# Three HGRN heads in emission order on three engines, and a decayed query moved to GpSimd

## The chip, the core and the metric

One core of a Trainium2 chip runs the whole program. The metric is the device time of one execution in microseconds, as the median of several runs. TensorE (PE) multiplies, VectorE (DVE), ScalarE (ACT) and GpSimd (POOL) do the elementwise work, and SyncE (SP) issues most of the DMAs.

## The reference

The network has two layers over 512 tokens of width 1024. The first layer runs sliding-window attention and four HGRN2 heads side by side, the second runs chunked attention, and each is followed by a gated convolutional FFN. The change touches the HGRN2 heads alone. For one head, with keys and values of width 128:

```python
f = lbh + (1.0 - lbh) * sigmoid(f_logit)          # forget gate
k = 1.0 - f
cum = cumsum(log(f), axis=block)                  # blocks of 32 tokens
q_dec, k_dec = q * exp(cum), k * exp(-cum)
k_end = k * exp(last - cum)
o_intra = causal(q_dec @ k_dec.T) @ v             # inside a block
state = blk_decay[..., None] * state + k_end.T @ v
o = o_intra + q_dec @ state                       # then RMSNorm and gate
```

## The kernel before

Activations lie with features on the partitions and the 512 tokens along the free side. A weight is split into a high and a low part, and a product is three matmuls (`mm3`, L248 to L250). One unit of weights is 128x1024 and serves a projection of 128 features (`feat`): eight steps of three matmuls. When a unit begins, the unit two behind it is prepared (`prep`): a DMA on SP, a cast on ScalarE (L216), a subtraction on VectorE (L217). The tile buffers let the scheduler do that earlier.

The projections are generators in a list. `fill(n)` runs n steps of them, and `need(name)` runs them until one is finished, which also runs the first step of the next one. So the matmuls of the projections are dealt out between the small matmuls of a head.

**One head, `hgrn(h)`.** `hgrn_in(h)` projects the forget gate and the query. `forget` works on the gate: tanh on ScalarE (L700), the gate (L701), the key 1-f on GpSimd (L702), a scan (L703 to L705) that makes the running product F of each block, a small table of block decays (L708 to L711), then for each of four groups of 128 tokens a reciprocal of F (L714) and a product with the key (L715), giving the decayed key `kd`. GpSimd then makes `f2` (L717) and `k2` (L684). `query` makes the decayed query `qd` (L722), a scaled copy `q2` of half of it (L684 on VectorE), and `kt` (L684 on GpSimd).

`hgrn(h)` itself, in the order of the code: eight steps of the list, which finish the next head's forget gate and begin its query; the scores inside a block (L743) and between blocks (L747, L749); the mask (L750, VectorE) and three copies (L756 and L757 on ScalarE, L758 on VectorE) into the tile `sz`, all of which write the same tile in this order; three steps; the transposes of `kt` (L763) and their copy into `keT` (L765, ScalarE); two steps; the state matmuls (L769), which read `keT`; the three states (L775, L777, VectorE); two steps, which finish the next head's query; the output matmuls (L781 from `sz`, L783 from the states); the squares (L788, ScalarE), the inverse root (L789 and L296 to L300, VectorE) and the scaling of the output (L792, ScalarE).

What sets the order is the framework's scheduler. It orders each engine's instructions by their place in the code and by when its own model thinks them ready, so a later instruction may go ahead of an earlier one that waits. The states and the copy into `keT` are marked for earlier issue. Inside a region `manual_schedule(engines=...)` the named engines issue in exactly the order in which the code emits; the other engines, and where outside instructions fall, stay the scheduler's. The kernel uses such a region for its opening already. An engine works through its list in order, and one that waits holds up what is listed behind it.

Of the kernel before, what the change touches and what calls it, by code (L numbers as in the profile page):

```python
# [23 lines left out]
AF = mybir.ActivationFunctionType  # L24
ALU = mybir.AluOpType
PSUM = bass.MemoryType.PSUM

P = 128
T = 512
NT = T // P  # L30
# [6 lines left out]
EPS = 1e-6  # L37
# [3 lines left out]
HB = 32  # L41
# [3 lines left out]
TOK = [slice(t * P, (t + 1) * P) for t in range(NT)]  # L45
# [103 lines left out]
class Net:  # L149
# [490 lines left out]
    def even(self, xs, ib):  # L640

        nc, tc = self.nc, self.tc
        with tc.tile_pool(name="ev", bufs=2) as ep:
# [34 lines left out]
            ob = [obt[h // 2][:, FH[h % 2]] for h in range(4)]  # L678
            mix = [None] * 8
            blk = lambda t: t.rearrange("p (b n) -> p b n", n=HB)  # L680
            quad = lambda t: t.rearrange("p (t b n) -> p t b n", b=P // HB, n=HB)

            def scaled(out, src, by, engine=nc.gpsimd):
                engine.tensor_mul(out, src, by.unsqueeze(3).to_broadcast(list(src.shape)))  # L684


            tabs = [ep.tile([P, NT, 16], F32, tag=f"tab{i}", bufs=1, name=f"tab{i}") for i in range(2)]
# [3 lines left out]
            def hgrn_in(h):  # L691

                ht = lambda i: self.hp.tile([P, D], F32, tag=f"h{i}", name=f"hg{h}{i}")
                h0, h1 = ht(2 * (h % 2)), ht(2 * (h % 2) + 1)
                f2, kk, F, kd = h0[:, FH[0]], h0[:, FH[1]], h1[:, FH[0]], h1[:, FH[1]]
                qd = tl("qd", "qd", 2)
                k2, q2 = (kk[:, z].rearrange("p (t b n) -> p t b n", b=2, n=HB) for z in (A, B))

                def forget(ps):
                    nc.scalar.activation(f2, ps, AF.Tanh, scale=0.5)  # L700
                    nc.vector.tensor_scalar(f2, f2, c1[:, h:h + 1], c0[:, h:h + 1], op0=ALU.mult, op1=ALU.add)  # L701
                    nc.gpsimd.tensor_scalar(kk, f2, -1.0, 1.0, op0=ALU.mult, op1=ALU.add)  # L702
                    nc.vector.tensor_copy(dd[:, ::HB], f2[:, ::HB])  # L703
                    nc.vector.memset(f2[:, ::HB], 0.0)
                    nc.vector.tensor_tensor_scan(F, f2, dd, 0.0, op0=ALU.mult, op1=ALU.add)  # L705

                    tab = tabs[h % 2]
                    nc.vector.tensor_copy(tab[:, :, 1::4], quad(F)[:, :, :, HB - 1])  # L708
                    nc.vector.tensor_mul(tab[:, :, 2:13:10], tab[:, :, 1:14:12], tab[:, :, 5:10:4])
                    nc.vector.tensor_mul(tab[:, :, 3:12:8], tab[:, :, 2:13:10], tab[:, :, 9:4:-4])  # L710
                    nc.vector.tensor_mul(tab[:, :, 15], tab[:, :, 3], tab[:, :, 13])  # L711

                    for t in range(NT):
                        nc.vector.reciprocal(kd[:, TOK[t]], F[:, TOK[t]])  # L714
                        nc.vector.tensor_mul(kd[:, TOK[t]], kd[:, TOK[t]], kk[:, TOK[t]])  # L715

                    nc.gpsimd.tensor_mul(blk(f2), blk(kd), blk(F)[:, :, HB - 1:].to_broadcast([P, T // HB, HB]))  # L717

                    scaled(k2, quad(f2)[:, :, 0:2], tab[:, :, 5:7])

                def query(ps):
                    nc.vector.tensor_mul(qd, ps, F)  # L722

                    scaled(q2, quad(qd)[:, :, 2:4], tabs[h % 2][:, :, 8:10], nc.vector)

                    scaled(quad(F), quad(f2), tabs[h % 2][:, :, 11:15])

                yield from self.feat(xs, forget)
                yield from self.feat(xs, query)
                heads[h] = (f2, kk, q2, F, kd, qd)  # L730

            heads = [None] * 4

            def hgrn(h):


                self.need(f"hg{h}")
                self.fill(8)
                ke, keT, q2, kt, kd, qd = heads[h]
                tab = tabs[h % 2]  # L740
                intra = self.bank("t", 2)
                for t in range(NT):
                    nc.tensor.matmul(intra[:, TOK[t]], kd[:, TOK[t]], qd[:, TOK[t]], start=True, stop=True)  # L743
                far = self.bank("s", 2)
                for t in range(NT):
                    o = t * P
                    nc.tensor.matmul(far[:, o:o + 64], ke[:, TOK[t]], quad(qd)[:, t, 1::2], start=True, stop=True)  # L747

                    nc.tensor.matmul(far[:, o + 64:o + P], keT[:, 64 * t:64 * t + P], q2[:, t], start=True, stop=True)  # L749
                nc.vector.copy_predicated(sz.rearrange("p (t n) -> p t n", n=P),  # L750
                                          cst[:, CC_HM:CC_HM + P].bitcast(I32).unsqueeze(1).to_broadcast([P, NT, P]),
                                          intra.rearrange("p (t n) -> p t n", n=P))

                scaled(quad(kd), quad(qd), tab[:, :, 0:4])
                s4, f4 = quad(sz), quad(far)
                nc.scalar.copy(s4[0:32, :, 1], f4[0:32, :, 0])  # L756
                nc.scalar.copy(s4[64:96, :, 3], f4[64:96, :, 1])  # L757
                nc.vector.tensor_copy(s4[0:64, :, 2:4], f4[0:64, :, 2:4])  # L758
                self.fill(3)

                ps = self.bank("t", 2)
                for t in range(NT - 1):
                    nc.tensor.transpose(ps[:, TOK[t]], kt[:, TOK[t]], self.ident)  # L763
                with self.tc.high_priority(AHEAD):
                    nc.scalar.copy(keT[:, 0:(NT - 1) * P], ps[:, 0:(NT - 1) * P])  # L765
                self.fill(2)
                po, pu = self.bank("po", 1), self.bank("s", 2)
                for t in range(NT - 1):
                    nc.tensor.matmul(pu[:, TOK[t]], keT[:, TOK[t]], ib[t][:, TOK[h]], start=True, stop=True)  # L769
                S = []  # L770
                with self.tc.high_priority(AHEAD):
                    for t in range(NT - 1):
                        S.append(ep.tile([P, P], F32, tag="S", bufs=3, name="S"))
                        if t == 0:
                            nc.vector.tensor_copy(S[0], pu[:, TOK[0]])  # L775
                        else:
                            nc.vector.scalar_tensor_tensor(S[t], S[t - 1], tab[:, t, 15:16], pu[:, TOK[t]],  # L777
                                                           op0=ALU.mult, op1=ALU.add)
                self.fill(2)
                for t in range(NT):  # L780
                    nc.tensor.matmul(po[:, TOK[t]], sz[:, TOK[t]], ib[t][:, TOK[h]], start=True, stop=t == 0)  # L781
                    if t:
                        nc.tensor.matmul(po[:, TOK[t]], kd[:, TOK[t]], S[t - 1], start=False, stop=True)  # L783

                ss, nv = self.small(4, "hs"), self.small(4, "hv")
                for t in range(NT):
                    j = self.sp.tile([P, D], BF16, tag="junk", bufs=1, name="junk")[:, 0:P]
                    nc.scalar.activation(j, po[:, TOK[t]], AF.Square, accum_out=ss[:, t:t + 1])  # L788
                nc.vector.tensor_scalar(nv, ss, -0.5 / P, -0.5 * EPS, op0=ALU.mult, op1=ALU.add)  # L789
                rs = self.rsqrt4(nv)  # L790
                for t in range(NT):
                    nc.scalar.activation(ob[h][:, TOK[t]], po[:, TOK[t]], AF.Copy, scale=rs[:, t:t + 1])  # L792


            rot = {}
# [82 lines left out]
            def gate(h):  # L878
                def turn(ps):
                    sl = tl("g", "sl", 1)  # L880
                    nc.scalar.activation(sl, ps, AF.Tanh, scale=0.5)
                    nc.vector.scalar_tensor_tensor(sl, sl, 1.0, ps, op0=ALU.add, op1=ALU.mult)
                    pt = self.bank("t", 2)
                    for t in range(NT):
                        nc.tensor.transpose(pt[:, TOK[t]], ob[h][:, TOK[t]], self.ident)
                    nc.vector.tensor_mul(sl, sl, pt)
                    mix[4 + h] = mx_tile(4 + h)
                    self.split(sl, *mix[4 + h], hgn[:, h:h + 1])
                return self.feat(xs, turn)
# [7 lines left out]
                self.later(f"qa{c}", rope(f"qa{c}", 0.125))  # L897
            for h in range(4):
                self.later(f"gate{h}", gate(h))
            for h in range(4):  # L900
                hgrn(h)

            def attention():
                work = [(c, g, i) for c in range(4) for g in range(2) for i in range(NT)]
# [245 lines left out]
```

## Time and profile before

| what | value |
|---|---|
| median of 3 runs | 1211.64 us (1211.58 to 1211.75) |
| the profiled execution: its time, its span | 1212.55 us, 1210.8 us |
| busy share of PE, DVE, ACT, POOL | 99%, 54%, 44%, 9% |
| mean granted TensorE clock | 0.998 |
| the HGRN stage, first to last score matmuls and outputs | about 52 to 116 us of the span |

The span is the time between the first and the last instruction of the profiled execution. A matmul's end is modelled, so the distance between starts tells its cost better than its length: 512 columns start about 0.23 us apart. Idle time counts for the end only where TensorE is idle, or where the end of the program waits.

### The profile page before, as it was taken

What the parts mean: (1) busy time and instruction counts of PE and PEld (TensorE: products, weight loads), DVE (VectorE), ACT (ScalarE), POOL (GpSimd) and SP (SyncE); (2) the same over time, 40 slices, a digit from 0 to 9 for tenths busy, and PEclk for the clock granted to TensorE, in tenths of its full rate; (3) what the DMA queues carried; (4) which work ended last, traced back from release to release, by engine and by line L of the source; (5) the groups of instructions that cost most, each with busy time, mean ns of one, the idle gap of its engine ahead of it and who ended that gap; (6) DMA issues with size and microseconds to landing.
All of it is one profiled execution on the core that took longest, in us unless ns stands there. A gap on an engine that the chain in (4) does not pass through costs nothing.

```text
span 1210.8 us, 15381 instructions
## 1 busy us (share of the span) xinstructions
PE 1195.8 (99%) x5789; PEld 979.3 (81%) x5789; DVE 656.1 (54%) x1356; ACT 534.5 (44%) x975; POOL 111.8 (9%) x120
## 2 busy tenths in 40 slices
PE   9999999999999999999999999999999999999997
PEld 5888777888888888888887777778888888888886
DVE  6887795654442244443547857747544422544434
ACT  5434675653332233333556656656533322333331
POOL 1231010500000000001420000004100000000011
PEclk9999999999999999999999999999999999999999
DMA  6414312233222332322233313222333223232211
GB/s 252 140 53 148 97 62 87 73 132 110 89 95 96 104 102 90 105 85 94 91 115 96 94 47 125 88 72 75 122 106 103 88 90 111 95 104 89 95 61 70
DMA packets 35611, 119.54 MB, mean 99 GB/s; under 512 B 4168, under 2 KB 4304, under 8 KB 35536
## 3 DMA queue, kind: packets, MB, share of 16 engines
q1 hardware_dynamic: 34944, 117.49, 29.5%
q8 instruction: 46, 0.75, 0.2%
q10 hardware_dynamic: 592, 1.05, 0.2%
q14 instruction: 29, 0.24, 0.1%
HBM read 115.12 MB, written 2.10 MB: 97 GB/s over the span
## 4 chain that ended last, share of the span: by engine, by line
PE 89%; DVE 3%; issue 3%; ACT 2%; POOL 2%; DMA 1%; SPq 0%; DVEq 0%; ACTq 0%; POOLq 0%
PE ps_mm L248 18%; PE ps_mm L250 18%; PE ps_mm L249 18%; PE ps_s L248 4%; PE ps_s L250 4%; PE ps_s L249 4%; PE ps_po L248 3%; PE ps_po L250 3%; PE ps_po L249 3%; PE ps_po L1030 2%; POOL hw L346 2%; PE ps_t L1019 1%; PE ps_mm L1084 1%; PE ps_s L1001 1%; PE ps_s L1002 1%
## 5 line engine op out<-in xcount | busy, mean ns | idle before, releaser
L217 DVE TENSOR_TENSOR wl<-wr,wh 128x1024 fp32r<-128x1024 f32 (+1 forms) x187 | 232.5, 1246 | 313.3 <-ACT wh L216 308.6
L216 ACT CAST wh<-wr 128x1024 fp32r<-128x1024 f32 x194 | 200.0, 1034 | 370.1 <-PE ps_mm L249 109.8
L248 PE MATMUL ps_mm<-xh,wh 128*128 128x512 f32 x608 | 242.6, 399 | 0.0
L250 PE MATMUL ps_mm<-xh,wl 128*128 128x512 f32 x608 | 238.0, 391 | 0.0
L249 PE MATMUL ps_mm<-xl,wh 128*128 128x512 f32 x608 | 237.8, 391 | 0.0
L250 PEld LDWEIGHTS ps_mm<-xh,wl 128*128 128x128 f32 x608 | 114.2, 188 | 23.4
L248 PEld LDWEIGHTS ps_mm<-xh,wh 128*128 128x128 f32 x608 | 114.5, 188 | 20.5
L249 PEld LDWEIGHTS ps_mm<-xl,wh 128*128 128x128 f32 x608 | 114.6, 188 | 20.2
L248 PE MATMUL ps_mm<-wh,ah 128*128 128x512 f32 x264 | 102.8, 389 | 0.0
L250 PE MATMUL ps_mm<-wh,al 128*128 128x512 f32 x264 | 102.7, 389 | 0.0
L249 PE MATMUL ps_mm<-wl,ah 128*128 128x512 f32 x264 | 102.7, 389 | 0.0
L561 POOL TENSOR_TENSOR y<-y,nw 128x512 f32<-128x512 f32 x16 | 22.2, 1395 | 675.6 <-ACT junk L314 675.6
L248 PE MATMUL ps_s<-xh,wh 128*128 128x512 f32 x208 | 80.9, 389 | 0.0
L249 PE MATMUL ps_s<-xl,wh 128*128 128x512 f32 x208 | 80.9, 389 | 0.0
L250 PE MATMUL ps_s<-xh,wl 128*128 128x512 f32 x208 | 80.9, 389 | 0.0
L1060 ACT ACTIVATE g<-g 128x512 f32<-128x512 f32 x44 | 27.8, 632 | 83.8 <-DVE g L1059 83.8
L250 PEld LDWEIGHTS ps_mm<-wh,al 128*128 128x128 f32 x264 | 49.6, 188 | 10.3
L249 PEld LDWEIGHTS ps_mm<-wl,ah 128*128 128x128 f32 x264 | 49.6, 188 | 10.3
L248 PEld LDWEIGHTS ps_mm<-wh,ah 128*128 128x128 f32 x264 | 49.6, 188 | 10.2
L1061 DVE TENSOR_TENSOR a<-ps_mm,g 128x512 f32<-128x512 f32 x32 | 22.1, 692 | 56.1 <-PE ps_mm L250 55.8
L1007 ACT ACTIVATE pr<-pr,m 128x128 f32<-128x128 f32 (+1 forms) x64 | 36.0, 562 | 33.8 <-DVE m L1006 33.3
L250 PEld LDWEIGHTS ps_s<-xh,wl 128*128 128x128 f32 x208 | 39.0, 188 | 8.1
(276 smaller groups left out, 2052.6 us busy)
## 6 DMA issues: line engine op xcount, KB each, us to landing
wr<-in_w SPq DMA_DIRECT2D x190, 512.0 KB, 3.5
nw<-in_nw SPq DMA_DIRECT2D x8, 512.0 KB, 3.7
bt<-in_relb SPq DMA_DIRECT2D x16, 256.0 KB, 3.2
x<-in_x SPq DMA_DIRECT2D x4, 512.0 KB, 8.3
h<-in_x SPq DMA_DIRECT2D x4, 512.0 KB, 4.0
wr<-in_w SPq DMA_DIRECT2D x8, 256.0 KB, 2.5
rope<-rope SPq DMA_DIRECT2D x20, 64.0 KB, 2.0
out<-h SPq DMA_DIRECT2D x4, 256.0 KB, 2.0
```

The lines of the kernel that those rows point to most:

```text
L216: nc.scalar.copy(hi[:, :n], raw[:, :n])
L217: (nc.gpsimd if i in POOL_LO else nc.vector).tensor_sub(lo[:, :n], raw[:, :n], hi[:, :n].bitcast(F32))
L248: mm(ps, a[0], b[0], start=start, stop=False, skip_group_check=skip)
L249: mm(ps, a[0], b[1], start=False, stop=False, skip_group_check=skip)
L250: mm(ps, a[1], b[0], start=False, stop=stop, skip_group_check=skip)
L346: nc.gpsimd.tensor_mul(hw, src, w)
L561: nc.gpsimd.tensor_mul(z, z, wy[:, FH[f]])
L1001: nc.tensor.matmul(ps[:, :w], q[g][:, TOK[i]], k[g][:, :w], start=True, stop=False)
L1007: nc.scalar.activation(p_, p_, AF.Exp, bias=m, accum_out=den)
L1030: nc.tensor.matmul(po[rows, j * P:], v[j][:, o:o + 64], pT[g][:, po_[j]:po_[j] + T - j * P], start=j == 0, stop=j == 3, skip_group_check=True)
L1060: nc.scalar.activation(g, g, AF.Gelu)
L1061: nc.vector.tensor_mul(a, pv, g)
```

## The change

1. The three heads 0, 1 and 2 run inside a region that fixes the emission order on PE, DVE and ACT. The step `need(f"hg{h + 1}")` now stands between the squares and the inverse root of head h. Head 3 runs as before, behind the region.
2. `forget` keeps the reciprocal and product of the first 128 tokens. The other three, with `f2` and `k2`, are put off into `rest`; for heads 1 to 3 it is called in `hgrn` of the head before, right behind the three states. For head 0 it is called at once.
3. `q2` is made on GpSimd instead of VectorE.

```diff
-            def scaled(out, src, by, engine=nc.gpsimd):
-                engine.tensor_mul(out, src, by.unsqueeze(3).to_broadcast(list(src.shape)))
+            def scaled(out, src, by):
+                nc.gpsimd.tensor_mul(out, src, by.unsqueeze(3).to_broadcast(list(src.shape)))
...
-                    for t in range(NT):
-                        nc.vector.reciprocal(kd[:, TOK[t]], F[:, TOK[t]])
-                        nc.vector.tensor_mul(kd[:, TOK[t]], kd[:, TOK[t]], kk[:, TOK[t]])
-
-                    nc.gpsimd.tensor_mul(blk(f2), blk(kd), blk(F)[:, :, HB - 1:].to_broadcast([P, T // HB, HB]))
-
-                    scaled(k2, quad(f2)[:, :, 0:2], tab[:, :, 5:7])
+                    def decay(ts):
+                        for t in ts:
+                            nc.vector.reciprocal(kd[:, TOK[t]], F[:, TOK[t]])
+                            nc.vector.tensor_mul(kd[:, TOK[t]], kd[:, TOK[t]], kk[:, TOK[t]])
+
+                    def rest():
+                        decay((1, 2, 3))
+                        nc.gpsimd.tensor_mul(blk(f2), blk(kd), blk(F)[:, :, HB - 1:].to_broadcast([P, T // HB, HB]))
+                        scaled(k2, quad(f2)[:, :, 0:2], tab[:, :, 5:7])
+
+                    decay((0,))
+                    if h:
+                        waiting.append(rest)
+                    else:
+                        rest()
...
-                    scaled(q2, quad(qd)[:, :, 2:4], tabs[h % 2][:, :, 8:10], nc.vector)
+                    scaled(q2, quad(qd)[:, :, 2:4], tabs[h % 2][:, :, 8:10])
...
-                self.need(f"hg{h}")
...
+                while waiting:
+                    waiting.pop()()
                 self.fill(2)
...
-                nc.vector.tensor_scalar(nv, ss, -0.5 / P, -0.5 * EPS, op0=ALU.mult, op1=ALU.add)
-                rs = self.rsqrt4(nv)
-                for t in range(NT):
-                    nc.scalar.activation(ob[h][:, TOK[t]], po[:, TOK[t]], AF.Copy, scale=rs[:, t:t + 1])
+                def norm():
+                    nc.vector.tensor_scalar(nv, ss, -0.5 / P, -0.5 * EPS, op0=ALU.mult, op1=ALU.add)
+                    rs = self.rsqrt4(nv)
+                    for t in range(NT):
+                        nc.scalar.activation(ob[h][:, TOK[t]], po[:, TOK[t]], AF.Copy, scale=rs[:, t:t + 1])
+                return norm
...
-            for h in range(4):
-                hgrn(h)
+            self.need("hg0")
+            E = mybir.EngineType
+
+            with self.tc.manual_schedule(engines={E.PE, E.DVE, E.Activation}):
+                for h in range(3):
+                    norm = hgrn(h)
+                    self.need(f"hg{h + 1}")
+                    norm()
+            hgrn(3)()
```

## Rows read from the trace of the kernel before

**Rows 1.** The page's first line, the page's line of busy time for TensorE and its weight loads, and two of its costliest groups (busy us and mean ns of one behind the bar, then idle before).

```profile
span 1210.8 us, 15381 instructions
...
PE 1195.8 (99%) x5789; PEld 979.3 (81%) x5789; DVE 656.1 (54%) x1356; ACT 534.5 (44%) x975; POOL 111.8 (9%) x120
...
L217 DVE TENSOR_TENSOR wl<-wr,wh 128x1024 fp32r<-128x1024 f32 (+1 forms) x187 | 232.5, 1246 | 313.3 <-ACT wh L216 308.6
L216 ACT CAST wh<-wr 128x1024 fp32r<-128x1024 f32 x194 | 200.0, 1034 | 370.1 <-PE ps_mm L249 109.8
```

**Rows 2.** What TensorE waited for over the whole run: who waited, for whom, us in total, times, longest us. The two rows that fall into the HGRN stage.

```profile
PE ps_po L783 <- DVE S L775: 2.1, 3, 0.9
...
PE ps_s L749 <- DVE hg L684: 0.9, 1, 0.9
```

**Rows 3.** TensorE in order of time, head 1 (start us, us, line, operation, count; in brackets the idle time before it and what ended it).

```profile
70.64 1.05 PE L743 MATMUL ps_t<-qd,hg 128*128 128x128 f32 x8
...
77.12 0.83 PE L769 MATMUL ps_s<-ib,hg 128*128 128x128 f32 x6
...
79.18 0.61 PE L781 MATMUL ps_po<-ib,sz 128*128 128x128 f32 x4
80.36 0.46 PE L783 MATMUL ps_po<-S,hg 128*128 128x128 f32 x2 [0.58 <-DVE S L775]
...
81.75 0.49 PE L783 MATMUL ps_po<-S,hg 128*128 128x128 f32 x2
...
88.01 1.05 PE L743 MATMUL ps_t<-qd,hg 128*128 128x128 f32 x8
```

**Rows 4.** TensorE in order of time, heads 0 and 3.

```profile
51.89 1.05 PE L743 MATMUL ps_t<-qd,hg 128*128 128x128 f32 x8
...
59.41 0.83 PE L769 MATMUL ps_s<-ib,hg 128*128 128x128 f32 x6
...
64.39 0.49 PE L783 MATMUL ps_po<-S,hg 128*128 128x128 f32 x2
...
113.92 0.61 PE L781 MATMUL ps_po<-ib,sz 128*128 128x128 f32 x4
...
115.40 0.48 PE L248 MATMUL ps_mm<-xh,wh 128*128 128x512 f32 x1
```

**Rows 5.** VectorE in order of time, from the last state of head 0 to the scan for head 2.

```profile
64.10 0.24 DVE L777 SCALAR_TENSOR_TENSOR S<-S,tab,ps_s 128x128 f32<-128x128 f32 x1
...
64.47 0.67 DVE L722 TENSOR_TENSOR qd<-ps_mm,hg 128x512 f32<-128x512 f32 x1
65.07 1.79 DVE L217 TENSOR_TENSOR wl<-wr,wh 128x1024 fp32r<-128x1024 f32 x1
...
67.54 1.02 DVE L789 TENSOR_SCALAR hv<-hs 128x4 f32<-128x4 f32 x1
68.60 0.17 DVE L296 TENSOR_SCALAR rs<-hv 128x4 int32<-128x4 int32 x1
...
73.83 0.54 DVE L701 TENSOR_SCALAR hg<-hg,fix 128x512 f32<-128x512 f32 x1
74.28 0.74 DVE L750 COPY_PREDICATED sz<-cst,ps_t 128x512 f32<-128x512 int32 x1
...
75.37 1.23 DVE L705 TENSOR_TENSOR_SCAN hg<-hg,dd 128x512 f32<-128x512 f32 x1
```

**Rows 6.** VectorE's groups by line and shape between 40 and 118 us (count, then busy us and mean ns of one).

```profile
L714 DVE RECIPROCAL hg<-hg 128x128 f32<-128x128 f32 x16 | 14.6, 934 | 0.0
...
L715 DVE TENSOR_TENSOR hg<-hg,hg 128x128 f32<-128x128 f32 x16 | 4.2, 271 | 0.0
```

**Rows 7.** ScalarE in order of time, heads 0 to 1.

```profile
70.57 1.14 ACT L792 ACTIVATE ob<-ps_po,rs 128x128 f32<-128x128 f32 x4 [4.09 <-DVE rs L300]
...
72.53 0.62 ACT L700 ACTIVATE hg<-ps_mm 128x512 f32<-128x512 f32 x1
75.11 0.26 ACT L756 COPY sz<-ps_s 32x128 f32<-32x128 f32 x1 [1.96 <-DVE dd L703]
...
75.98 0.48 ACT L765 COPY hg<-ps_t 128x384 f32<-128x384 f32 x1 [0.34 <-PE ps_t L763]
...
82.33 0.28 ACT L788 ACTIVATE junk<-ps_po 128x128 bf16<-128x128 f32 x1 [2.15 <-PE ps_po L783]
...
83.53 0.28 ACT L788 ACTIVATE junk<-ps_po 128x128 bf16<-128x128 f32 x1
```

**Rows 8.** GpSimd in order of time, heads 0 to 1.

```profile
64.69 1.09 POOL L717 TENSOR_TENSOR hg<-hg 128x512 f32<-128x512 f32 x1 [6.96 <-DVE hg L715]
65.86 2.68 POOL L684 TENSOR_TENSOR hg<-hg,tab 128x256 f32<-128x256 f32 x2
71.78 1.05 POOL L684 TENSOR_TENSOR hg<-qd,tab 128x512 f32<-128x512 f32 x1 [3.24 <-PE ps_t L743]
74.45 0.62 POOL L702 TENSOR_SCALAR hg<-hg 128x512 f32<-128x512 f32 x1 [1.63 <-DVE hg L701]
```

**Rows 9.** TensorE in order of time at the two ends of the run: the first matmuls, and the last one.

```profile
1.20 3.17 PE L436 MATMUL ps_s<-scratch 128*128 128x512 bf16 x7 [1.20 <-DVE warm L430]
...
1203.28 0.39 PE L250 MATMUL ps_po<-wh,al 128*128 128x512 f32 x1
```

**Rows 10.** Busy time by stretch, one of 1 us behind the last matmul (length, then PE, PEld, DVE, ACT, POOL busy us with their counts; then the granted TensorE clock, the DMA share and GB/s).

```profile
1207.00:1208.00 1.00, 0.00 (x0) 0.00 (x0) 0.71 (x2) 0.00 (x0) 0.00 (x0) 0.50 0.08 33
```

More of the change, by code (lines that the diff above doesn't have):

```diff
@@ L732, in even @@
             heads = [None] * 4
+            waiting = []
             def hgrn(h):
-                self.need(f"hg{h}")
                 self.fill(8)
```

## The prediction, made before the changed kernel was run

> **What bounds the kernel now.** I read the page first: TensorE is busy for 1195.8 of 1210.8 us [rows 1], so only what lets it stand still, or makes it do more, can move the end. Next I read its waits. In the HGRN stage it waits three times for the first state of a head (2.1 us) and once for `q2` (0.9 us) [rows 2]. Then I read the engines in order of time.
>
> In head 1 the output matmuls begin at 79.18 and stop 0.58 us for a state [rows 3]; their last pair begins at 81.75, which is 2.57 us later (the pair's own length and a projection matmul let ahead of it cancel). Head 3 does the same outputs in 1.48 us, with no wait [rows 4]. So heads 1 and 2 lose 1.09 us each, and head 0, whose way from L769 to the last pair is 4.98 us instead of 4.63 [rows 3, 4], loses 1.44. With the wait for `q2` that is 4.5 us: **the most that the change can win**. The reader is to see in [rows 3] what is free of waits: 6.48 us from L743 to L769, 4.63 - 1.09 = 3.54 from L769 to the end of the outputs, and 6.26 from there to the next L743. A head needs 16.28 us of TensorE and takes 17.37 now.
>
> **What the change does to the lists.** It moves the states ahead of three of four reciprocal pairs; at 0.934 + 0.271 us a pair [rows 6] this ends the wait for the states. But the fixed order brings more with it than that. The scheduler now lets the mask L750 of head h go right behind the next head's gate L701 (0.45 us later), ahead of the scan [rows 5]. In the code's order the mask of head h stands behind the whole of the next head's `forget`: scan, four table operations, the first reciprocal and product, and a weight subtraction L217. On ScalarE the two copies into `sz` wait for the mask (L756 starts 0.09 us behind its end [rows 5, 7]), and L765, which makes `keT`, stands behind them and can no longer pass. TensorE's state matmuls L769 read `keT`, and all later matmuls queue behind them. So **a new wait stands where TensorE had none**: L769 for L765. Moreover the next head's tanh L700 stands behind the scaling L792 of the head before, and that behind the inverse root, a weight cast and the put-off reciprocals. This closes a ring, and each head takes the ring's time if that is over 16.28 us.
>
> **The ring, step by step**, from the end of a head's third state (0) to the same point of the next.
> - Three pairs of reciprocal and product, each product waiting for its reciprocal: 3 x 1.2 = 3.6; `qd`, 0.6: VectorE at 4.2 [rows 5, 6].
> - The next L217 needs its cast on ScalarE, which now stands behind four squares. The last output pair starts at 1.5 (3.54 us behind L769's start, less its own length, the states ending some 1.8 us behind that start), the squares 0.58 us later, 0.40 each [rows 3, 7], the cast takes 1.03 [rows 1]: 4.75. L217 (1.25) is done at 6.0 to 6.4.
> - The inverse root: L789 starts at 67.54 but takes 1.02, ending 0.02 us behind GpSimd's chain that started with L717 at 64.69 and ends at 68.54 [rows 5, 8]. That chain lasts 3.85 us; with `q2` in it some 0.5 more (it shares 2.68 us with L217 and the old `q2` for two operations [rows 8], a pure 512-column one takes 1.05). Started at 3.65, it ends at 8.0, so L296 starts at 8.1 and L792 1.97 later [rows 5, 7]: 10.1. GpSimd's L684 behind L743 (1.05 us [rows 8]) falls into this at about 9.0 and may hold up the small operations once: 10.1 to 11.1. I take 10.5, since its neighbours L701 and L789 were both held.
> - L792 for 1.02, tanh 0.65, gate L701 at 12.2 [rows 7]. Gate to scan 1.54, with the key on GpSimd between [rows 5, 8]; scan 1.25; table 0.7 at 0.2 each, as the inverse root's small ones; reciprocal and product 1.2; L217 1.15; mask 0.74: 18.8.
> - L756 and L757 with their starts 0.7, L765 0.5: L769 at 20.05. Six matmuls and three states, 1.8: **21.9 us**. Bounds: 19.8, if GpSimd holds up nothing; 22.9, if each hold is full.
>
> So heads 1 and 2 cost 21.9 - 17.37 = 4.5 us more each (2.4 to 5.5), TensorE standing 5.6 us before L769.
>
> **Head 0.** Its `qd` is ready before L743 at 51.89, which reads it without a wait [rows 2, 4], and the wait for `q2` goes, as GpSimd makes it right behind `k2`, about when L749 wants it (cost nothing to 0.4; now 0.9 is lost). The gate's last matmul starts four projection matmuls ahead of L743, so the tanh can start at 51.4 and L701 at 52.1; GpSimd's chain holds up gate, key and scan, so the scan starts at 54.6 to 57.0, taken 55.6. The same steps as above, 6.25, give L769 at 61.9 where it stands at 59.41 [rows 4]; the outputs then end 3.54 later at 65.4, against 64.39 plus nothing, as defined above: +1.0 (0 to +2.4).
>
> **Further terms.** (a) Weights: in the region, casts and subtractions go at their place in the code, two units (16 us) ahead instead of as far as the buffers reach. Their DMAs are issued on SP as buffers fall free, up to some us later; a load has two units of cover, so nothing; without that cover a late one would add to the cast, and so to ScalarE's whole list. Two preparations move behind the region, 2 x 1.25 us of VectorE, which is busy for 54% of the run [rows 1]: nothing. (b) VectorE loses `q2`; it is in the sum. (c) Head 3 is outside; its states are early, its 1.48 stays. (d) **The clock.** TensorE's granted clock is 0.50, the lower level, in the stretch at 1207 us, 3.3 us behind the end of the last matmul at 1203.67 [rows 9, 10]; 5.6 us of standing are longer than that. At the run's start seven matmuls of 512 columns take 3.17 us [rows 9], 0.45 each, where 0.23 is usual. A restart at the lower level for about as long as there costs half of 3.2, 1.6 us, in full behind head 2's wait; behind head 1's only the six state matmuls (0.6) are on the ring. From 0 to 4, I take 1.0, since it also moves L684 out of the inverse root.
>
> Beside the row at the run's end stands a rule of the Trainium skill, "TensorE: Matmul & The Clock Gate", Part 1: the lower clock is the default and activity releases it. By it the clock falls in both waits and the last term would be 2.2, the sum 1.2 higher; by the waits of under 1 us in [rows 2] alone it would be 0. No run here has a wait of that length in the middle.
>
> A rule that speaks against moving `q2`: the Trainium skill, "GPSIMD Engine Reference", 4.1 Engine selection, calls GpSimd about half as fast as VectorE on two-input operations. The rows have 1.05 us on GpSimd (L684 at 71.78) against 0.67 on VectorE (L722) for 512 columns, a factor of 1.6 [rows 5, 8]; by the rule's factor `q2` would take 0.67 instead of 0.5, and the sum would be 0.3 higher.
>
> **The sum.** 1.0 + 2 x 4.5 + 1.0 = 11.0 us. On the profiled execution: span 1210.8 to 1221.8; its own time, 1.75 above its span, 1212.55 to 1223.55. That run is 0.9 above the median of three, so the median goes from 1211.64 to **1222.6**. The terms' bounds give 0 + 4.8 + 0 = 4.8 to 2.4 + 11.0 + 4.0 = 17.4: 1216.4 to 1229.0; all at once are unlikely, 1217 to 1227 holds most.
>
> **Rivals.**
> - *The states' wait goes and nothing takes its place: faster.* The place is the mask: if it runs by 4.6 us behind L743 (6.48 less 1.9 for the copies), L769 doesn't wait. That needs L701 1.2 us ahead of L743, where it stands 3.2 behind L743 in head 1 now [rows 3, 5]; or a fixed order that doesn't bind L765. Then all 4.5 us but 0.4 are won: 1207.5. For it speaks that the longest wait of today is just what the moved states remove; against it the list, by which mask, copies and `keT` can't pass. 0.14.
> - *The ring is shorter than I sum, near today's 17.37 us, and win and loss cancel*: GpSimd holds up nothing, and casts and squares overlap better. It would need 2 us less than my lower bound of 19.8. 1210 to 1216, middle 1213. 0.10.
> - *Each wait also pays the clock in full, and GpSimd's holds add up:* over 1227, about 1229. 0.06.
> - *The change doesn't do what it says*, outside work falling between the region's: a weight preparation in VectorE's list adds 1.25 us a head at most. It stays within the forecast's range.
>
> **How the numbers follow.** The forecast has 0.70. A measurement can tell about 0.2%, 2.4 us, from no change. Faster by more: the first rival and a little of the second, 0.15. Within: half of the second, 0.06. Slower by more: the rest, 0.79. Of the range 1212 to 1228, the first rival and the ends of two others are left out, 0.2.
>
> **What would show it.** In TensorE's waits the row for L783 on L775 is gone, and L769 waits for ScalarE's L765, about 2 to 4.5 us in head 0 and 4 to 6 in heads 1 and 2, or less if the ring is short. L743 of heads 1, 2, 3 stand about 22 us apart from head 1 on. VectorE's mask runs behind L217; L765 starts within 0.7 us of the mask's end. L749 doesn't wait. The granted clock falls in one or both waits. I am wrong if L769 never waits, or if L756 starts ahead of a mask in the list's order; and if the wait is at L781 the ring bites at the outputs and not at `keT`.

## The result, and the profile after

The changed kernel takes 1223.61 us (median of 5 runs, 1223.28 to 1225.54), the kernel before 1211.58 beside it: a ratio of 1.0101 (95% interval 1.0090 to 1.0112), 12.0 us slower. The forecast was 1222.6, in a range of 1212 to 1228.

The page's first line and its line of busy time (before: [rows 1]):

```profile
span 1221.5 us, 15369 instructions
...
PE 1200.9 (98%) x5789; PEld 984.4 (81%) x5789; DVE 656.0 (54%) x1352; ACT 533.6 (44%) x975; POOL 111.1 (9%) x124
```

The span grew by 10.7 us, of which 5.1 are TensorE *busy* for longer with the same 5789 instructions, and 5.6 are TensorE standing. What TensorE waited for in the HGRN stage (before: [rows 2]):

```profile
PE ps_s L780 <- ACT hg L776: 9.8, 3, 3.8
```

The rows for the states and for `q2` are gone. In their place the state matmuls (L769 before, L780 now) wait in each of the three heads for ScalarE's copy into `keT` (L765 before, L776 now). In order of time, the score matmuls (L754) and the state matmuls of the heads (before: [rows 3, 4]):

```profile
50.90 1.05 PE L754 MATMUL ps_t<-qd,hg 128*128 128x128 f32 x8
60.32 1.38 PE L780 MATMUL ps_s<-ib,hg 128*128 128x128 f32 x6 [2.78 <-ACT hg L776]
71.78 1.05 PE L754 MATMUL ps_t<-qd,hg 128*128 128x128 f32 x8
...
82.24 1.65 PE L780 MATMUL ps_s<-ib,hg 128*128 128x128 f32 x6 [3.82 <-ACT hg L776]
...
94.79 1.05 PE L754 MATMUL ps_t<-qd,hg 128*128 128x128 f32 x8
104.61 1.30 PE L780 MATMUL ps_s<-ib,hg 128*128 128x128 f32 x6 [3.18 <-ACT hg L776]
...
116.08 1.05 PE L754 MATMUL ps_t<-qd,hg 128*128 128x128 f32 x8
```

From scores to scores the heads now take 20.88, 23.01 and 21.29 us, where before they took 18.75, 17.37 and 17.38 (51.89, 70.64 and 88.01 in [rows 3, 4], head 3 at 105.39): +11.7 in sum. The stage begins 1.0 us earlier than in the profiled execution of before, which gives the 10.7 of the span. That 1.0 belongs to that one execution: the other profiles below with eight steps ahead of the scores have their first scores at 50.55 to 51.18. So the two profiles, put on the same start, differ by 11.7, about what the medians do.

Why the copy is late shows on VectorE and ScalarE, head 1 (before: [rows 5, 7]):

```profile
76.06 1.23 DVE L705 TENSOR_TENSOR_SCAN hg<-hg,dd 128x512 f32<-128x512 f32 x1
...
79.23 1.22 DVE L217 TENSOR_TENSOR wl<-wr,wh 128x1024 fp32r<-128x1024 f32 x1
80.36 0.71 DVE L761 COPY_PREDICATED sz<-cst,ps_t 128x512 f32<-128x512 int32 x1
...
83.93 0.29 DVE L786 COPY S<-ps_s 128x128 f32<-128x128 f32 x1 [1.79 <-PE ps_s L780]
```

```profile
81.17 0.25 ACT L767 COPY sz<-ps_s 32x128 f32<-32x128 f32 x1 [5.71 <-DVE sz L761]
...
81.71 0.48 ACT L776 COPY hg<-ps_t 128x384 f32<-128x384 f32 x1
```

The mask (L761) stands behind the next head's scan, table, reciprocal and weight subtraction. ScalarE does nothing for 5.71 us, since the first copy into `sz` wants the mask, and the copy that TensorE needs is listed behind it, though its transposes were done at 77.0. And the longer busy time, in stretches behind the three waits (length, busy us of PE, PEld, DVE, ACT, POOL, then the granted clock):

```profile
60.00:64.00 4.00, 3.68 (x12) 3.16 (x13) 2.38 (x7) 0.27 (x1) 0.00 (x0) 0.58 0.32 123
82.00:88.00 6.00, 5.76 (x21) 5.18 (x22) 4.07 (x9) 0.19 (x1) 0.00 (x0) 0.50 0.20 76
104.00:108.00 4.00, 3.39 (x12) 2.91 (x13) 2.36 (x6) 0.53 (x2) 0.00 (x0) 0.63 0.53 185
```

The first and the third stretch hold both levels. Inside each of the three there are 2 us at 0.50, the lower level (62 to 64, 82 to 84, 106 to 108): the clock fell behind all three waits, and TensorE's 512 columns then start 0.43 us apart instead of 0.23.

### The profile page after: what moved, and what is told of

The parts are those of the page before. It is cut to its first block, busy times and chain, and to the rows that moved or that the text cites. A ratio compares the mean times of both kernels' runs of the same rounds, so it can differ in the third digit from the quotient of the medians.

```text
span 1221.5 us, 15369 instructions
## 1 busy us (share of the span) xinstructions
PE 1200.9 (98%) x5789; PEld 984.4 (81%) x5789; DVE 656.0 (54%) x1352; ACT 533.6 (44%) x975; POOL 111.1 (9%) x124
## 4 chain that ended last, share of the span: by engine, by line
PE 88%; DVE 3%; ACT 3%; issue 3%; POOL 2%; DMA 0%; DVEq 0%; ACTq 0%; POOLq 0%
PE ps_mm L248 18%; PE ps_mm L249 18%; PE ps_mm L250 18%; PE ps_s L248 4%; PE ps_s L249 4%; PE ps_s L250 4%; PE ps_po L249 3%; PE ps_po L248 3%; PE ps_po L250 3%; PE ps_po L1053 2%; POOL hw L346 2%; PE ps_t L1042 1%; PE ps_mm L1107 1%; PE ps_s L1024 1%; PE ps_s L1025 1%
## 5 line engine op out<-in xcount | busy, mean ns | idle before, releaser
L217 DVE TENSOR_TENSOR wl<-wr,wh 128x1024 fp32r<-128x1024 f32 (+1 forms) x187 | 230.4, 1234 | 312.7 <-ACT wh L216 308.0
L561 POOL TENSOR_TENSOR y<-y,nw 128x512 f32<-128x512 f32 x16 | 22.2, 1395 | 675.6 <-ACT junk L314 675.6
L248 PEld LDWEIGHTS ps_s<-xh,wh 128*128 128x128 f32 x208 | 39.1, 188 | 8.1
```

Source lines behind the costliest of these rows:

```text
L217: (nc.gpsimd if i in POOL_LO else nc.vector).tensor_sub(lo[:, :n], raw[:, :n], hi[:, :n].bitcast(F32))
L248: mm(ps, a[0], b[0], start=start, stop=False, skip_group_check=skip)
L561: nc.gpsimd.tensor_mul(z, z, wy[:, FH[f]])
```

## The experiments

The theory: the fixed order makes the mask late on VectorE, and ScalarE's list passes this on to `keT`. The rivals: the copy is late for a cause of its own; one of the other two parts costs the time; the lower clock costs it. Times of before beside these runs: 1211.41, 1211.55 and 1211.43 us.

**The copies into `sz` behind `keT`'s copy (e1_copies_last).**

```diff
-                nc.scalar.copy(s4[0:32, :, 1], f4[0:32, :, 0])
-                nc.scalar.copy(s4[64:96, :, 3], f4[64:96, :, 1])
...
                     nc.scalar.copy(keT[:, 0:(NT - 1) * P], ps[:, 0:(NT - 1) * P])
+                nc.scalar.copy(s4[0:32, :, 1], f4[0:32, :, 0])
+                nc.scalar.copy(s4[64:96, :, 3], f4[64:96, :, 1])
```

> The two ScalarE copies into sz (L767, L768) are written behind keT's copy (L776); nothing else moves. Theory (L780 waits because ScalarE's fixed order holds keT's copy behind the mask): L776 runs right behind the transposes, some 4 us earlier; L780 starts without a wait; the first state copy L786 no longer waits for L780 but for the mask and L769 ahead of it on VectorE, about 2.4 us earlier than now; what is late next is sz and the states, 1 to 2 us in front of L794. The ring from state copy to state copy goes from 22 to about 18.3 us (2.4 from the copy, about 1.5 from squares that no low clock delays), so about 10 us less than the changed kernel: 1213.5 us, 1211 to 1216. The granted clock stays at full speed. Rival (VectorE's own order sets the ring; the copy is only the last to be seen): L780's wait goes, and as much waits at L794: 1220 to 1224 us.

1216.49 us, ratio 1.0042 (1.0030 to 1.0055): 7.1 us of the 12.0 come back. TensorE's waits, and VectorE and ScalarE in head 1:

```profile
PE ps_po L794 <- DVE S L788: 6.0, 3, 3.5
```

```profile
77.94 0.72 DVE L761 COPY_PREDICATED sz<-cst,ps_t 128x512 f32<-128x512 int32 x1
...
79.11 0.27 DVE L786 COPY S<-ps_s 128x128 f32<-128x128 f32 x1
```

```profile
72.94 0.48 ACT L774 COPY hg<-ps_t 128x384 f32<-128x384 f32 x1
```

`keT` (now L774) is there 4.5 us before the mask starts (73.42 against 77.94) and L780 doesn't wait: that the copy was held by its place in ScalarE's list is shown. But the states are still behind the mask, and the wait moved to the outputs. The ring from first state to first state is 20.0 us (59.10 to 79.11), not the 18.3 expected.

**The forget chain behind the mask (e2_forget_later).** `self.fill(8)` becomes `self.fill(6)`, and the `self.fill(3)` behind the copies `self.fill(5)`.

> Two of the eight fill steps at the head of each head are moved behind the score matmuls (6 and 5 in place of 8 and 3), so the next head's forget chain and weight subtraction are written behind the mask instead of ahead of it. Theory (the mask is late because forget's chain, 4 to 5 us, lies ahead of it in VectorE's fixed order): the mask follows the inverse root, L776 follows ScalarE's copies without a wait for it, L780 does not wait; the forget chain now stands ahead of the first state copy, which comes 17 to 18 us after the state copy of the head before, in place of 22; L794 waits about 1 us for states. About 12 us less than the changed kernel: 1211.5 us, 1208 to 1214. Rival (keT's copy is late for another reason: the transposes, or GpSimd's decayed keys): L780 waits as now, 1221 to 1225 us. Rival (the chain only changes its place in the ring, and the states are as late as they are now): L794 waits 4 us, 1219 to 1223 us.

1216.81 us, ratio 1.0048 (1.0034 to 1.0061). L780 doesn't wait; L796 waits twice 2.1 us for the first state. The ring from first state to first state is 19.37 us (60.04 to 79.41), not 17 to 18. In e1 and e2 the wait at L780 went as told, and both rings came out some 2 us too long. VectorE and GpSimd side by side, behind head 0:

```profile
66.90 0.58 DVE L804 TENSOR_SCALAR hv<-hs 128x4 f32<-128x4 f32 x1
67.52 0.54 DVE L296 TENSOR_SCALAR rs<-hv 128x4 int32<-128x4 int32 x1
68.09 0.97 DVE L298 TENSOR_TENSOR rt<-rs,hv 128x4 f32<-128x4 f32 x1
69.10 0.97 DVE L299 TENSOR_TENSOR rt<-rt,rs 128x4 f32<-128x4 f32 x1
70.11 0.16 DVE L300 SCALAR_TENSOR_TENSOR rs<-rt,rs 128x4 f32<-128x4 f32 x1
```

```profile
65.97 1.48 POOL L684 TENSOR_TENSOR hg<-hg,tab 128x256 f32<-128x256 f32 x1
67.42 0.61 POOL L684 TENSOR_TENSOR hg<-qd,tab 128x256 f32<-128x256 f32 x1
68.00 1.05 POOL L684 TENSOR_TENSOR hg<-hg,tab 128x512 f32<-128x512 f32 x1
69.01 1.04 POOL L684 TENSOR_TENSOR hg<-qd,tab 128x512 f32<-128x512 f32 x1
```

Four small instructions of the inverse root each end within 0.03 us of a GpSimd multiplication's end (67.45, 68.03, 69.05, 70.05); the first without one beside it takes 0.16. The root takes 4.47 us (66.90 to the mask's start at 71.37) where an undisturbed one of the changed kernel, at 93.09, took 2.16. This became a theory of its own, tried in e9 below.

**The region taken away (e3_no_region).** Only the `with` line goes.

> The changed kernel with the region of fixed order taken away: the states still come ahead of the reciprocals in the program, the decayed queries are still on GpSimd, but the scheduler orders TensorE, VectorE and ScalarE. Theory (the fixed order costs the time, the two other parts bring some back): the waits at L780 stay under 1 us, heads are 16.5 to 17.5 us apart, 1209 us, 1206.5 to 1212. Rival (the reordered reciprocals or GpSimd's queries themselves cost the time): 1216 us or more, with the wait in front of L780 or L754.

1212.07 us, ratio 1.0008 (0.9999 to 1.0016). So the fixed order costs all of it; the other two parts bring nothing, against 2.4 us expected. Its longest wait in the stage:

```profile
PE ps_s L760 <- POOL hg L684: 2.0, 1, 2.0
```

That is head 0, for `q2` on GpSimd. And `qd` follows the first state by 1.83 us, as it did in before (64.47 in [rows 5], the state at 62.64): without the region the scheduler runs most of the reciprocals ahead of the states again, whatever the code's order, so the reordering by itself changes little.

**Matmuls without use in the waits (e4_keep_busy).**

```diff
+                if h < 3:
+                    for _ in range(11):
+                        nc.tensor.matmul(po, xs[0][0][:, TOK[0]], xs[0][0], start=True, stop=True)
```

> Eleven matmuls of 512 columns without use (x's high half by itself into the bank that the output's matmuls clear later) stand in front of L780 in each of the three heads, 2.5 us at 0.23 us each, less than the shortest wait that stands there now (2.78 us). The outputs do not depend on them. Theory (half of the loss is the lower clock that each wait brings): the granted clock stays at full speed, L780's starts move by less than 0.3 us behind their releasers, what is left of its waits is 0.3 to 1.3 us, the stretch behind L780 runs at full speed and gives back about 5 us: 1218.5 us, 1217 to 1220.5. Rival (the ring on VectorE and ScalarE sets the time, the clock costs nothing): the clock stays at full speed and the time stays at 1222 to 1224.5 us.

1221.96 us, ratio 1.0087 (1.0074 to 1.0101): 1.65 us come back, so the rival is nearly right. The same stretches as above (heads 0, 1, 2):

```profile
60.00:64.00 4.00, 3.97 (x28) 3.65 (x28) 2.83 (x6) 0.04 (x1) 0.00 (x0) 1.00 0.26 103
82.00:86.00 4.00, 4.00 (x17) 3.53 (x18) 2.41 (x6) 0.00 (x0) 0.00 (x0) 0.61 0.24 99
104.00:108.00 4.00, 4.00 (x28) 3.68 (x29) 3.06 (x7) 0.19 (x2) 0.00 (x0) 1.00 0.65 217
```

The clock held behind heads 0 and 2; behind head 1 TensorE came to the wait earlier, still stood 2.69 us, and the clock fell again. From state matmuls to state matmuls the heads take 21.71 and 22.03 us (60.09, 81.80, 103.83), against 21.92 and 22.37: where the clock slows TensorE in front of the next wait, the wait only gets shorter. Behind head 2, where no long wait follows, the way from state matmuls to the next scores falls from 11.47 to about 9.9 us (the first of these eight score matmuls has no record, so its start, about 113.7, is reckoned from L758 behind it). Some of that is lost again: head 3's state matmuls, which don't wait in the changed kernel, now wait 0.48 us.

**The decayed queries alone (e5_q2_alone).** The kernel before, with `q2` on GpSimd.

> The kernel before with one part of the change alone: the decayed queries on GpSimd instead of VectorE; the scheduler orders everything. Theory (this part neither brings nor costs much; in the kernel without the region L760 of head 0 waited 2.0 us for GpSimd, 1.1 more than before, and nothing else changed): the wait of 0.9 us for the queries in head 0 becomes about 2, heads stay 17.4 us apart: 1212.4 us, 1211.5 to 1213.5. Rival (VectorE is relieved by what the queries took, and that shortens its ring): heads 16.9 us apart, 1210.5 us.

1212.90 us, ratio 1.0010 (1.0001 to 1.0019), as expected: the wait of 0.9 us in head 0 becomes 2.29, and heads 1 to 3 stay 17.35 and 17.38 us apart. Not all of the 1.35 us over before need be the wait's: the runs go from 1211.24 to 1214.71 us, and the last section has what goes with that.

**VectorE left out of the region (e6_no_dve_order).** `engines={E.PE, E.Activation}`.

> The changed kernel with VectorE left out of the region of fixed order; TensorE and ScalarE keep it. Theory (the order on VectorE, with forget's chain ahead of the mask, is what makes the mask and behind it ScalarE's copies late; ScalarE's order by itself holds nothing if the mask comes early): the waits at L780 fall from 9.8 us to under 2 in sum, heads are 17.3 to 18.5 us apart, 1213 us, 1211 to 1215.5. Rival (ScalarE's order suffices for the loss): waits of 3 us at L780 stay, 1219 to 1224 us.

1210.82 us, ratio 0.9994 (0.9985 to 1.0003): all is won back, more than I expected. TensorE's waits in the stage:

```profile
PE ps_po L796 <- DVE S L786: 1.4, 2, 0.7
...
PE ps_po L796 <- DVE S L788: 0.8, 3, 0.3
```

L780 doesn't wait though ScalarE keeps the fixed order. The states come late again (L796), so the win that the changed order was to bring doesn't come either. The mask runs 4.06 us behind the scores (71.78, scores at 67.72), ahead of the scan; in the changed kernel it was 8.58 (80.36, 71.78). It is VectorE's order that does the harm.

**The inverse root on GpSimd (e7_root_gpsimd)**, on top of e2_forget_later.

```diff
-    def rsqrt4(self, nv):
-        v = self.nc.vector
+    def rsqrt4(self, nv, v=None):
+        v = v or self.nc.vector
...
-            v.scalar_tensor_tensor(y, t, 1.5, y, op0=ALU.add, op1=ALU.mult)
+            v.tensor_scalar(t, t, 1.0, 1.5, op0=ALU.mult, op1=ALU.add)
+            v.tensor_mul(y, y, t)
...
-                    nc.vector.tensor_scalar(nv, ss, -0.5 / P, -0.5 * EPS, op0=ALU.mult, op1=ALU.add)
-                    rs = self.rsqrt4(nv)
+                    nc.gpsimd.tensor_scalar(nv, ss, -0.5 / P, -0.5 * EPS, op0=ALU.mult, op1=ALU.add)
+                    rs = self.rsqrt4(nv, nc.gpsimd)
```

> The kernel with the forget chain behind the mask (e2_forget_later), and with the inverse root of each head's norm (scale, seed, three rounds on 128 x 4) on GpSimd instead of VectorE, its fused last step as two instructions. Theory (VectorE's small instructions of the root are held by GpSimd's multiplications: 4.47 us for the root in e2_forget_later where an undisturbed one of the changed kernel took 2.16, and 1.80 instead of 1.22 for the weight subtraction ahead of it; that is why e2_forget_later's ring is 19.4 us): without the root VectorE's ring is about 15 us, TensorE's 16.3 us bound it, heads are 16.3 to 17 us apart: 1210 us, 1208.5 to 1213. Rival (GpSimd's many small instructions are long or hold VectorE elsewhere, and the bank of the outputs comes free late): a wait of 2 us or more in front of L794 or L754, 1214 to 1219 us.

1222.72 us, ratio 1.0087 (1.0073 to 1.0101): a miss by 12.7 us. The root's instructions mix with GpSimd's products, so it ends at 71.0, hardly earlier than in e2 (71.45), and the change's own fault comes back in another place. ScalarE and VectorE behind head 0:

```profile
71.03 1.14 ACT L808 ACTIVATE ob<-ps_po,rs 128x128 f32<-128x128 f32 x4 [7.06 <-POOL rs L301]
72.05 0.24 ACT L768 COPY sz<-ps_s 32x128 f32<-32x128 f32 x1
```

```profile
72.58 0.41 DVE L770 COPY sz<-ps_s 64x256 f32<-64x256 f32 x1 [4.70 <-ACT sz L769]
```

The scaling of the head before stands ahead of the copies in ScalarE's fixed list, and VectorE's copy behind them waits 4.70 us for a root that it doesn't need. The ring stays 19.3 us. The scores' waits for GpSimd also grew, to 4.8 us in sum, and head 3's root, on GpSimd too, lets a matmul of the attention wait 1.6 us. The profiled execution took 1220.03 us, the other three 1222.40 to 1223.72, so 2 to 3 us of the median stand in no trace. This run couldn't tell whether the holds matter.

**One step more ahead of the outputs, in the kernel before (e8_one_step, e12_one_step_again).** The `self.fill(2)` in front of the output matmuls becomes `self.fill(3)`.

> The kernel before with three fill steps instead of two between the state matmuls and the outputs, the step taken from what need() runs behind the head. Theory (the kernel before loses 2.1 us where L783 waits for the states, 0.93, 0.58 and 0.58 us; one step of 0.7 us more ahead of it covers them but for 0.2): these waits go, 1209.7 us, 1209 to 1210.6. Rival (VectorE's ring of 17.36 us sets the period, not the place of the wait): the same waits at L783 or elsewhere, 1211 to 1212 us.

> The kernel of e8_one_step once more, for its profile (the first run's profiled execution had TensorE at half its rate throughout and tells nothing of the waits). Theory (the step covers what L783 waits): no waits of 0.6 to 0.9 us for the states at L783; since the first run gave only 0.5 us, 1.1 to 1.6 us of the 2.1 must then be seen elsewhere between the heads. Rival (VectorE's ring of 17.36 us sets the distance of heads 1 to 3): the heads stay 17.3 us apart and the wait stands at L783 or moves to L743 or L749. Time 1211.0 us, 1210.5 to 1211.5.

1211.04 and 1210.96 us, ratios 0.9994 (0.9985 to 1.0003) and 0.9996 (0.9987 to 1.0005): no change that can be measured. In the second run's profile:

```profile
PE ps_po L783 <- DVE S L775: 0.9, 3, 0.3
PE ps_po L783 <- DVE S L777: 0.8, 3, 0.3
```

The waits got smaller one by one and more in number, and the scores stay 17.35 us apart (68.72, 86.07, 103.41). The rival was right: something other than the place of that wait sets 17.36 us in the kernel before.

**Without GpSimd's products (e9_no_products)**, on top of e2_forget_later: L721 and the four calls of `scaled` are left out.

> The kernel with the forget chain behind the mask (e2_forget_later), without GpSimd's five multiplications per head (L721 and the four of scaled); the matmuls that read their results read what stands in those tiles, so the outputs of these heads leave the decay factors out. Theory (these multiplications hold VectorE's instructions that run beside them: the root took 4.47 us in e2_forget_later where 2.16 were seen without a hold, and the weight subtraction ahead of it 1.80 instead of 1.22): root 2.2 us, subtraction 1.2, the ring falls from 19.4 to about 16.5 us, heads are 16.5 us apart, 1210.5 us, 1209 to 1212.5. Rival (the holds stand where VectorE would wait for ScalarE's copies or for the projection anyway): the ring stays over 18.5 us, 1214 to 1217 us.

1207.65 us, ratio 0.9968 (0.9956 to 0.9979). VectorE:

```profile
59.38 0.28 DVE L781 COPY S<-ps_s 128x128 f32<-128x128 f32 x1
...
65.64 0.16 DVE L799 TENSOR_SCALAR hv<-hs 128x4 f32<-128x4 f32 x1
65.84 0.17 DVE L296 TENSOR_SCALAR rs<-hv 128x4 int32<-128x4 int32 x1
...
75.80 0.28 DVE L781 COPY S<-ps_s 128x128 f32<-128x128 f32 x1
```

The root takes 2.05 us (65.64 to the mask at 67.69) instead of 4.47, the ring 16.42 instead of 19.37, and no wait of TensorE in these heads is left. 2.4 of the 2.95 us are the root's; the rest fits the weight subtraction, 1.21 against 1.80. The run also takes away what waited for the products themselves (0.26 to 0.42 us at L760 per head in the region of e2), so it bounds the holds from above, but only the root got that much shorter.

**VectorE alone in the region (e10_dve_only).** `engines={E.DVE}`.

> The changed kernel with the region of fixed order on VectorE alone; TensorE's order comes out as in the changed kernel, ScalarE's is the scheduler's, which puts keT's copy ahead of the two copies into sz. Theory (VectorE's order makes the ring of about 20 us, and ScalarE's order behind the late mask adds the rest, as in the run with the two copies behind keT's): no wait at L780, waits of 2 to 3.5 us at L794 for the states, heads 19.5 to 20 us apart, 1216 us, 1214 to 1217.5. Rival (VectorE's order does no harm by itself, only both together): 1210 to 1213 us.

1216.44 us, ratio 1.0041 (1.0028 to 1.0054): the time is as expected, and L780 doesn't wait. The rest came out less even than expected: the waits at L794 are 0.74, 2.10 and 3.92 us, for the last copy into `sz` rather than for the states, and from first state to first state VectorE takes 18.65 and 20.47 us. TensorE's only waits in this stage are then:

```profile
PE ps_po L794 <- DVE sz L769: 6.8, 3, 3.9
```

So the 12.0 us have two shares: 5.0 from VectorE's order alone (1216.44 against 1211.43), and 7.2 more when ScalarE and TensorE are fixed as well (1223.61), which by themselves cost nothing (e6). e1, which undoes only ScalarE's part by two lines, lands on the same 1216.5.

**VectorE left out, and one step more (e11_no_dve_step).** e6's line and e8's line together.

> The changed kernel with VectorE left out of the region (e6_no_dve_order, 1210.82 us), and one more fill step ahead of the outputs (3 in place of 2, taken from what need() runs behind the head). Theory (what that kernel still loses are waits of 1.4 and 0.8 us for the states at L796; a step of 0.7 us more covers them): 1209.0 us, 1208.3 to 1210.2, faster than the kernel before by 0.2%. Rival (VectorE's ring of 17.7 us sets the heads' distance; the wait only changes its place): 1210.5 to 1211.5 us.

1209.31 us (1208.92 to 1209.50), ratio 0.9981 (0.9972 to 0.9990): faster than both kernels. TensorE's scores (L754) start at 50.74, 67.13, 84.46 and 101.87. Head 0 takes 16.39 us, against 18.05 in e12, and that is all of the 1.65 us between the medians of the two. Heads 1 and 2 still take 17.33 and 17.41, with 0.3 us waits at L796 left. So the time was as expected, the reason only in part.

## Why the prediction was right

**The wait that goes and the wait that comes.** Both came as told: no wait at the outputs or at L749, and the state matmuls wait for `keT`'s copy, which starts 0.64 us behind the mask's end (81.71 against 81.07; 0.7 foretold). e1, e6 and e10 show the cause as the prediction put it: order on VectorE, passed on by order on ScalarE. The condition that the first rival named also holds: it asked for the mask by 4.6 us behind the scores, and e6, where it starts at 4.06, has no wait at the state matmuls.

**The ring, step by step**, from the end of head 0's third state (62.79; rows of VectorE, ScalarE and GpSimd, beside those above):

```profile
62.06 0.73 DVE L788 SCALAR_TENSOR_TENSOR S<-S,tab,ps_s 128x128 f32<-128x128 f32 x2
...
66.27 0.68 DVE L733 TENSOR_TENSOR qd<-ps_mm,hg 128x512 f32<-128x512 f32 x1
68.36 1.57 DVE L217 TENSOR_TENSOR wl<-wr,wh 128x1024 fp32r<-128x1024 f32 x1 [1.41 <-ACT wh L216]
...
70.92 0.17 DVE L296 TENSOR_SCALAR rs<-hv 128x4 int32<-128x4 int32 x1
...
74.55 0.55 DVE L701 TENSOR_SCALAR hg<-hg,fix 128x512 f32<-128x512 f32 x1 [1.70 <-ACT hg L700]
...
84.26 0.73 DVE L788 SCALAR_TENSOR_TENSOR S<-S,tab,ps_s 128x128 f32<-128x128 f32 x2
...
91.42 1.74 DVE L217 TENSOR_TENSOR wl<-wr,wh 128x1024 fp32r<-128x1024 f32 x1 [2.27 <-ACT wh L216]
```

```profile
72.89 1.14 ACT L807 ACTIVATE ob<-ps_po,rs 128x128 f32<-128x128 f32 x4 [4.56 <-DVE rs L300]
```

```profile
68.81 2.04 POOL L684 TENSOR_TENSOR hg<-hg,tab 128x512 f32<-128x512 f32 x1
```

| point | foretold | after |
|---|---|---|
| `qd` done | 4.2 | 4.16 |
| L217 done | 6.0 to 6.4 | 7.1 |
| L296 starts | 8.1 | 8.13 |
| scaling (L792, now L807) starts | 10.5 (10.1 to 11.1) | 10.10 |
| gate L701 | 12.2 | 11.76 |
| mask done | 18.8 | 18.28 |
| state matmuls | 20.05 | 19.45 |
| third state done | 21.9 | 22.2 |

In this ring the bound from GpSimd was the one that held: its chain ends at 70.85 (8.06, foretold 8.0), and L296 starts behind it, so the lateness of L217, behind late squares, cost nothing. From head 1 to head 2 it was the other way round: GpSimd's chain is done at 92.08, 7.1 behind that head's third state (84.99), L217 only at 93.16, and L296 starts at 93.28, 8.29 behind. The prediction had only the first of the two causes, and that the other came out as long is luck. I let one hold too many into the root (0.4), and the way from the state matmuls to the last state took 1 us more than foretold (2.75, foretold 1.8), since TensorE ran at the lower clock. The two nearly cancel. State matmuls are 21.92 and 22.37 us apart, +4.2 and +5.0 for the 2 x 4.5.

**Head 0.** The last output pair starts at 65.40, foretold 65.4, but that is chance, since the head begins 1.0 us earlier in this execution than in that of before. Counted from the head's first scores the state matmuls come at 9.42 (foretold 10.0) and the last output pair at 14.50 (foretold 13.5): this term was 2.0 and not 1.0. The prediction priced a lower clock behind the waits of heads 1 and 2 alone. It fell behind head 0's wait too, and the way from state matmuls to last output pair took 5.08 us, where 3.54 was foretold and e4, with the clock held, has 3.50. This 1.5 us isn't added to the total: it shortens head 1's wait.

**The clock**: 1.0 foretold (0 to 4). e4 gives 1.65 for the two of three falls that it took away; the 1.6 behind head 2 that the prediction worked out and then shaded measures about 1.6 (11.47 against 9.9). This term was mis-sized by some 0.6 us.

**TensorE standing 5.6 us** in heads 1 and 2 was wrong as a size: 3.82 and 3.18. The ring is the same, but at the lower clock TensorE's 16.28 us of work took about 18.1 and 19.2 of it (21.92 - 3.82, 22.37 - 3.18). Most of the 5.1 us of more busy time stand there, ahead of the next wait, which they only shorten. The 16.28 itself was well read: in e9, where TensorE doesn't wait, the heads are 16.37 to 16.43 us apart.

**`q2`**: 0.5 us on GpSimd foretold, 0.62 measured. That GpSimd makes it about when L749 wants it holds in the changed kernel. In e2, which has the fixed order too, it comes 0.26 to 0.42 us late, and in e3 and e5, without it, 2.0 and 2.3 us in head 0.

**The sum**, 11.0: 10.7 from profile to profile, 12.0 between the medians. The stage itself took 11.7 us more: 1.9 up to the state matmuls of head 0, 4.2 and 5.0 from there to those of heads 1 and 2, and 0.6 up to the scores of head 3, where the clock's 1.6 stands against the 1.1 won at the outputs. The prediction took the profile of before to be 0.9 us slow all along its run; it lost about that much ahead of the stage, and the run after didn't. So the nearness of 11.0 and 10.7 is partly chance; 11.7 is the number to hold it against.

**Open:** what sets 17.36 us per head in the kernel before. Neither the wait's place (e12) nor `q2` (e5) does. Its trace has a ring of just this length:

```profile
90.03 1.25 DVE L217 TENSOR_TENSOR wl<-wr,wh 128x1024 fp32r<-128x1024 f32 x1 [2.14 <-ACT wh L216]
```

From the L217 of the head before (72.68) VectorE works without a stop until the inverse root ends at 87.89, 15.21 us. Then it stands 2.14 us for a weight cast, which is listed on ScalarE behind the scaling L792 and so behind that same root; together 17.35. e12 has the same wait. No run took it away, so this is read and not shown.

## What to carry to other kernels

A fixed order fixes every pair on the engine, not only the pair that one wants turned round: go through each engine's list and ask which short instruction, one that the list of another engine waits for, now stands behind a long chain. Here leaving one of three engines to the scheduler (one word of the edit) was worth 12.8 us, and undoing it on the engine that only passes the delay on was worth 7. When a wait closes a ring, price the ring and not the wait: a lower clock or useful work in front of the wait changes where the time is seen, not how much it is.

## What the hardware showed beyond that

**Small VectorE instructions are held by GpSimd's, one by one.** In e2 instructions on 128 x 4 that take 0.16 us take 0.54 to 0.97 and end with a GpSimd multiplication, four in a row; without the multiplications (e9) all take 0.16 to 0.17. The Trainium skill, "SBUF — State Buffer", Who interferes with whom, has a port pair of VectorE and GpSimd as an exclusive lock on which the later one blocks fully. These rows agree, down to operands of four columns; which of the instructions hold each other was read from the trace, not tried one at a time.

**When the clock falls** can't be told from the wait's length alone. It fell behind waits of 0.87 (e7, head 2), 1.45 (e2, head 3), 1.93 (e1), 2.29 (e5) and 2.69 us (e4), and not behind waits of 2.02 (e3), 2.08 (e2, head 1) or 2.10 (e10). In e5 the wait ended at 54.20, the clock was still 1.00 up to 56, and 0.57 on average from 56 to 60. e3 and e5 have runs near 1211.3 us with a mean granted clock of 0.999, and others at 1214.1 to 1214.7 with 0.995. So what the late `q2` costs seems to hang on whether the clock falls; where it fell in those others isn't shown, since only one execution of each was profiled.
